# The last second product of the last MLP over 256, 128 and 128 tokens instead of 256 and 256

## The chip, the cores and the metric

The kernel runs on one core of a Trainium2 chip. The metric is the device time of one execution in microseconds (us), taken as the median of several runs. Before the change it is 2286.32 us (three runs, 2286.13 to 2287.78).

## The reference

Two layers over 1024 tokens of width 1024. The first mixes tokens by stick-breaking attention and a gated recurrence, the second by a convolution module; each is followed by an RMS-normed MLP with a squared ReLU, and a last RMS norm gives the output.

```python
def squared_relu_mlp(u, w1, w2):
    return jnp.square(jax.nn.relu(u @ w1)) @ w2
...
for layer in range(DEPTH):
    u = rmsnorm(h, norm_mix_g[layer])
    h = h + mixer(u)
    u = rmsnorm(h, norm_ffn_g[layer])
    h = h + squared_relu_mlp(u, w_ff1[layer], w_ff2[layer])
return rmsnorm(h, final_norm_g)
```

The MLP goes from 1024 to 4096 columns and back. The last norm needs, for each token, the sum of squares over all 1024 columns of the finished `h`.

## The kernel before

Activations lie transposed: 128 columns of the model on the partitions, tokens along the free dimension, so `h` is eight tiles `ht[hf][n]` (n = 0 to 7) of 128 x 512 for each half `hf` of the tokens. Every matrix is cut into panels of 128 output columns. `panel` (L100) loads one 512 KB panel into `wraw` (two buffers, queue of SyncE) and splits it into a rounded part and a remainder, `whl`: ScalarE writes the first (L110), VectorE the second (L111). `whl` has three buffers. Activations are split in the same way. `gemm` (L114) then makes three products for each of the 8 blocks of 128 rows of the contraction, L121 to L123, each of them a weight load of 128 x 128 and a matmul over the tokens; a whole panel is 24 matmuls. The same weights go in twice, at L121 and L122.

An MLP (`mlp`, L694) runs over its 32 hidden panels in four groups of eight: eight panels of the first product, then eight panels of the second product over the group's eight hidden tiles `hid`, each added into `ht` by VectorE. Only in the last MLP (layer 1, second half of the tokens), in its last group, the second product is different (L738 to L750): it goes over 256 tokens first and the other 256 after that. Panels 0 to 3 of its weights are split ahead of time into tiles of their own (`held`, tiles `w2`) and stay; panels 4 to 7 go through the three buffers of `whl`, and the second pass begins with 7, 6 and 5, which still lie there, and loads 4 a second time for its last place.

After each pass, `final` (L869) norms and writes these tokens. `colsum_sq` squares the tiles on ScalarE (`sq`, L193) and adds them on VectorE (`acc`, L195), all but the last square; `stats` (L125) sums over partitions by small matmuls against ones (L140, result `st`), makes 1/sqrt in a few small instructions on VectorE and GpSimd (L143 to L149) and spreads it over the partitions with matmuls against the identity (L153, result `stb`); a matmul of plain float32 operands is two records in the profile. Then VectorE scales each tile by norm and gain (L895) and ScalarE's queue issues its output DMA (L896). In the last pass GpSimd takes three of the eight tiles (L881, L892), with their DMAs on SyncE's queue, from a copy of `stb` (`rbc`, L885).

What stands in which order on an engine is decided by a scheduler when the program is built, with raised priority for splits, additions and the norm; each engine then runs its list strictly in order. DMA issues stand in the list of the engine that issues them.

Of the kernel before, what the change touches and what calls it, by code (L numbers as in the profile page):

```python
# [18 lines left out]
H = 512  # L19
KT = D // P  # L20
# [34 lines left out]
def kernel(  # L55
# [44 lines left out]
    def panel(src, n, hl=None):  # L100

        raw = wp.tile([P, KT * P], F32, tag="wraw", name="wraw", bufs=2)
        to = raw[:, :n]
        nc.sync.dma_start(to if len(src.shape) == 2 else to.rearrange("p (g c) -> p g c", g=src.shape[1]), src)
        if hl is None:
            t = wp.tile([P, 2, KT * P], F32R, tag="whl", name="whl")
            hl = t[:, 0], t[:, 1]
        hi, lo = hl
        with tc.high_priority(offset=PRIO):
            ACT.activation(hi[:, :n], raw[:, :n], AF.Copy)  # L110
            DVE.tensor_tensor(lo[:, :n], raw[:, :n], hi[:, :n].bitcast(F32), ALU.subtract)  # L111
        return hi, lo

    def gemm(ps, hl, mov, koff=0, start=True, stop=True):  # L114

        n = len(mov)
        whi, wlo = hl
        for k in range(n):
            c = slice((k + koff) * P, (k + koff + 1) * P)
            hi, lo = mov[k]  # L120
            PE.matmul(ps, whi[:, c], hi, start=start and k == 0, stop=False)  # L121
            PE.matmul(ps, whi[:, c], lo, start=False, stop=False)  # L122
            PE.matmul(ps, wlo[:, c], hi, start=False, stop=stop and k == n - 1)  # L123
# [79 lines left out]
    def utile(name):  # L203
        return up.tile([P, 2, H], F32R, tag="u", name=name)

    def parts(ts):
        return [(t[:, 0], t[:, 1]) for t in ts]
# [421 lines left out]
    def hs(hf):  # L629
        return lambda k: ht[hf][k]  # L630
# [42 lines left out]
    def mm():  # L673
        return late[3].tile([P, H], F32, tag="mm2", name="mm2", bufs=4) if late else \
            pm.tile([P, H], F32, tag="mm", name="mm")
# [18 lines left out]
    def mlp(layer, hf, u, last=None):  # L694

        held = {}
        w2 = lambda n, hl=None: panel(w_ff2[layer, n, :, f0 * P:(f0 + GF) * P], GF * P, hl)  # L700
        for f0 in range(0, FT, GF):
            hid = []
            for f in range(f0, f0 + GF):
                hl = panel(w_ff1[layer, f], D)
                ps = mm()
                gemm(ps, hl, u)
                with tc.high_priority(offset=PRIO):
                    if late:
                        t = late[0].tile([P, H], F32, tag="relu", name="relu")
                        hh = late[1].tile([P, 2, H], F32R, tag="hid", name="hid")  # L710
                        s = late[0].tile([P, H], F32, tag="sqr", name="sqr")
                    else:
                        t = wk.tile([P, H], F32, tag="raw", name="relu", bufs=2)
                        hh = utile("hid")
                        s = wk.tile([P, H], F32, tag="raw", name="sqr", bufs=2)
                    ACT.activation(t, ps, AF.Relu)  # L716
                    ACT.activation(hh[:, 0], t, AF.Square)  # L717
                    ACT.activation(s, t, AF.Square)  # L718
                    DVE.tensor_tensor(hh[:, 1], s, hh[:, 0].bitcast(F32), ALU.subtract)  # L719
                hid.append(hh)  # L720
                if last is not None and f >= FT - 4:
                    n = f - FT + 4
                    held[n] = [utile("w2").rearrange("p a b -> p (a b)") for _ in range(2)]
                    w2(n, held[n])
                yield
            if last is not None and f0 == FT - GF:
                break
            for n in range(KT):
                hl = w2(n)
                ps = mm()  # L730
                gemm(ps, hl, parts(hid))
                d = hs(hf)(n)
                with tc.high_priority(offset=PRIO):
                    DVE.tensor_tensor(d, d, ps, ALU.add)  # L734
                yield
        if last is None:
            return
        for q in range(2):  # L738
            tk = slice(q * H // 2, (q + 1) * H // 2)
            order = (7, 6, 5, 0, 1, 2, 3, 4) if q else range(KT)  # L740
            for n in order:
                if n > 3 and (q == 0 or n == 4):
                    held[n] = w2(n)
                ps = mm()[:, :H // 2]
                gemm(ps, held[n], [(hi[:, tk], lo[:, tk]) for hi, lo in parts(hid)])
                d = hs(hf)(n)[:, tk]
                with tc.high_priority(offset=PRIO):
                    DVE.tensor_tensor(d, d, ps, ALU.add)
                yield
            last(tk, order)  # L750
# [10 lines left out]
    def first_norm():  # L761
        assert all(("o", n) in done for n in range(KT))
        ms.append(mlp(0, 0, mlp_norm(0, 0)))
# [4 lines left out]
    for name in TOKENS.split():  # L768
        f, n = name[0], name[1:]
# [15 lines left out]
        else:  # L785
            f, n, hf = name[:-2], int(name[-2]), "ab".index(name[-1])
# [136 lines left out]
    steps(m)  # L923
    ug = norm(0, V_MIX + 8)
    m = mlp(0, 1, ub)
    steps(m, 8)
    ys = glu_conv(0, ug, m, 0)
# [3 lines left out]
    pw(cu, 0)  # L931
    ua = mlp_norm(1, 0)
    m = mlp(1, 0, ua)
    ys = glu_conv(1, ug, m, 3)
    cu = ln_silu(ys)
# [68 lines left out]
```

## Time and profile before

| what | value |
| --- | --- |
| median of three runs | 2286.32 us |
| the profiled execution, whole | 2286.64 us |
| its span, first to last instruction | 2284.9 us |
| TensorE matmul, busy | 2256.3 us, 99% |
| TensorE weight load, busy | 1893.1 us, 83% |
| VectorE, ScalarE, GpSimd, busy | 66%, 40%, 4% |
| mean granted TensorE clock | 0.997 |
| second product of the last group, 256 and 256 tokens | about 2227 to 2274.6 us of the span |

The profile names PE for TensorE's matmuls, PEld for its weight loads, DVE for VectorE, ACT for ScalarE, POOL for GpSimd; SPq and ACTq are DMA issues on the queues of SyncE and ScalarE. A row of the timeline gives the start in us, the length in us, the engine, the line, the operation, output<-input, sizes, and xN where N instructions that follow each other are merged; in brackets the idle time ahead of it and what ended it. A row of the groups gives busy time in us and mean ns of one instruction. A matmul's recorded length contains its way through the array, so matmuls overlap each other in the records; how fast they follow each other is read from their starts.

### The profile page before, as it was taken

How to read it: one execution, taken by the hardware profiler on the slowest of the kernel's cores; microseconds unless marked ns; L12 is line 12 of the kernel's file. 1: busy time of each engine (PE TensorE's matmuls, PEld its weight loads, DVE VectorE, ACT ScalarE, POOL GpSimd, SP SyncE). 2: the span in 40 equal slices, each digit the busy share in tenths (PEclk: the TensorE clock that was granted, in tenths of full speed). 3: DMA queues.
4: the chain of work that ended last, by engine and by line, in shares of the span. 5: the costliest groups of instructions: out<-in, count | busy, mean ns of one | idle time of the engine just before them, and what ended most of it. 6: DMA issues, size and time to landing. Idle time of an engine off the chain costs nothing.

```text
span 2284.9 us, 27492 instructions
## 1 busy us (share of the span) xinstructions
PE 2256.3 (99%) x10780; PEld 1893.1 (83%) x10780; DVE 1505.3 (66%) x2179; ACT 922.2 (40%) x1453; POOL 82.5 (4%) x167
## 2 busy tenths in 40 slices
PE   8999999998999999999999999999999999999998
PEld 7887888887888888888888888888888888888888
DVE  7776777777343453469999876899997646433343
ACT  6544444545442344342414353442324534342341
POOL 1100010100000000000000000000000000000000
PEclk9999999999999999999999999999999999999999
DMA  5221122422343333332333333232332332423241
GB/s 174 70 63 47 46 73 80 128 88 71 114 138 98 93 101 92 99 95 94 100 95 100 94 100 93 93 100 94 100 94 93 102 93 92 138 92 102 93 138 47
DMA packets 70832, 217.96 MB, mean 95 GB/s; under 512 B 7984, under 2 KB 14256, under 8 KB 70704
## 3 DMA queue, kind: packets, MB, share of 16 engines
q1 hardware_dynamic: 59216, 197.71, 27.7%
q10 hardware_dynamic: 10208, 16.41, 2.2%
q0 software_dynamic: 1280, 2.10, 0.4%
q8 instruction: 84, 1.38, 0.2%
q14 instruction: 44, 0.36, 0.0%
HBM read 205.70 MB, written 8.39 MB: 94 GB/s over the span
## 4 chain that ended last, share of the span: by engine, by line
PE 97%; DVE 2%; ACT 1%; issue 0%; DMA 0%; POOL 0%; SPq 0%; POOLq 0%; ACTq 0%
PE mm L121 27%; PE mm L122 27%; PE mm L123 27%; PE av L443 2%; PE wtr L434 1%; PE pa L121 1%; PE pa L123 1%; PE pa L122 1%; PE pg L122 1%; PE pg L123 1%; PE pg L121 1%; PE zs L540 1%; PE z L415 1%; PE z L414 1%; PE st L140 1%; DVE ke L421 0%
## 5 line engine op out<-in xcount | busy, mean ns | idle before, releaser
L111 DVE TENSOR_TENSOR whl<-wraw,whl 128x1024 fp32r<-128x1024 f32 (+2 forms) x371 | 445.7, 1201 | 322.9 <-ACT whl L110 319.1
L110 ACT ACTIVATE whl<-wraw 128x1024 fp32r<-128x1024 f32 (+2 forms) x371 | 385.2, 1039 | 645.2 <-PE mm L123 522.6
L121 PE MATMUL mm<-u,whl 128*128 128x512 f32 x1456 | 571.8, 394 | 8.9 <-ACT u L279 6.1
L122 PE MATMUL mm<-u,whl 128*128 128x512 f32 x1456 | 570.8, 392 | 0.0
L123 PE MATMUL mm<-u,whl 128*128 128x512 f32 x1456 | 569.8, 391 | 0.0
L121 PE MATMUL mm<-hid,whl 128*128 128x512 f32 (+1 forms) x1024 | 391.6, 383 | 0.0
L122 PE MATMUL mm<-hid,whl 128*128 128x512 f32 (+1 forms) x1024 | 391.3, 383 | 0.0
L123 PE MATMUL mm<-hid,whl 128*128 128x512 f32 (+1 forms) x1024 | 390.8, 383 | 0.0
L837 DVE SCALAR_TENSOR_TENSOR y<-a,vec,y 128x512 f32<-128x512 f32 x480 | 345.1, 750 | 4.2
L121 PEld LDWEIGHTS mm<-u,whl 128*128 128x128 f32 x1456 | 273.9, 188 | 65.5 <-ACT u L279 6.8
L122 PEld LDWEIGHTS mm<-u,whl 128*128 128x128 f32 x1456 | 274.0, 188 | 55.2 <-DVE u L280 1.2
L123 PEld LDWEIGHTS mm<-u,whl 128*128 128x128 f32 x1456 | 274.0, 188 | 54.9
L123 PEld LDWEIGHTS mm<-hid,whl 128*128 128x128 f32 x1024 | 192.5, 188 | 37.4
L121 PEld LDWEIGHTS mm<-hid,whl 128*128 128x128 f32 x1024 | 192.5, 188 | 37.3
L122 PEld LDWEIGHTS mm<-hid,whl 128*128 128x128 f32 x1024 | 192.5, 188 | 37.2
L734 DVE TENSOR_TENSOR ht<-ht,mm 128x512 f32<-128x512 f32 x120 | 82.3, 687 | 199.3 <-PE mm L123 199.1
L716 ACT ACTIVATE relu<-mm 128x512 f32<-128x512 f32 x128 | 76.5, 598 | 326.1 <-PE mm L123 325.8
L421 DVE TENSOR_TENSOR_SCAN ke<-ke 128x128 f32<-128x128 f32 (+5 forms) x64 | 86.4, 1353 | 24.9 <-POOL ke L418 24.7
L719 DVE TENSOR_TENSOR hid<-sqr,hid 128x512 fp32r<-128x512 f32 x128 | 87.7, 686 | 4.1 <-ACT sqr L718 4.1
L717 ACT ACTIVATE hid<-relu 128x512 fp32r<-128x512 f32 x128 | 79.6, 622 | 0.1
L718 ACT ACTIVATE sqr<-relu 128x512 f32<-128x512 f32 x128 | 79.6, 622 | 0.0
L145 POOL TENSOR_TENSOR st_r<-st_m,nhalf 128x4 f32<-128x4 f32 (+1 forms) x21 | 24.1, 1149 | 1229.2 <-DVE st_m L143 1229.2
(227 smaller groups left out, 2501.2 us busy)
## 6 DMA issues: line engine op xcount, KB each, us to landing
wraw<-w_ff SPq DMA_DIRECT2D x257, 512.0 KB, 3.5
wraw<-w_in SPq DMA_DIRECT2D x46, 512.0 KB, 3.5
wraw<-w_glu SPq DMA_DIRECT2D x32, 512.0 KB, 3.5
wraw<-w_pw SPq DMA_DIRECT2D x16, 512.0 KB, 3.5
xk<-xT SPq DMA_DIRECT2D x16, 256.0 KB, 5.1
oraw<-o_dram ACTq DMA_DIRECT2D x16, 256.0 KB, 3.3
ht<-xT ACTq DMA_DIRECT2D x16, 256.0 KB, 4.0
wraw<-w_out SPq DMA_DIRECT2D x8, 512.0 KB, 3.6
```

The source lines that it names most:

```text
L110: ACT.activation(hi[:, :n], raw[:, :n], AF.Copy)
L111: DVE.tensor_tensor(lo[:, :n], raw[:, :n], hi[:, :n].bitcast(F32), ALU.subtract)
L121: PE.matmul(ps, whi[:, c], hi, start=start and k == 0, stop=False)
L122: PE.matmul(ps, whi[:, c], lo, start=False, stop=False)
L123: PE.matmul(ps, wlo[:, c], hi, start=False, stop=stop and k == n - 1)
L421: DVE.tensor_tensor_scan(kr, kr, kr, 1.0, ALU.mult, ALU.min)
L716: ACT.activation(t, ps, AF.Relu)
L717: ACT.activation(hh[:, 0], t, AF.Square)
L718: ACT.activation(s, t, AF.Square)
L719: DVE.tensor_tensor(hh[:, 1], s, hh[:, 0].bitcast(F32), ALU.subtract)
L734: DVE.tensor_tensor(d, d, ps, ALU.add)
L837: DVE.scalar_tensor_tensor(y, a[:, j:j + H], w(j), y, ALU.mult, ALU.add)
```

## The change

The second pass over 256 tokens is cut in two passes over 128. Each has its own eight additions, norm and output DMAs. Panel 4 is loaded again for the end of the second pass, as before, and is then used first in the third; panel 5 is loaded again for the end of the third.

```diff
-        for q in range(2):
-            tk = slice(q * H // 2, (q + 1) * H // 2)
-            order = (7, 6, 5, 0, 1, 2, 3, 4) if q else range(KT)
+
+        for tk, order, loads in ((slice(0, H // 2), range(KT), (4, 5, 6, 7)),
+                                 (slice(H // 2, 3 * H // 4), (7, 6, 5, 0, 1, 2, 3, 4), (4,)),
+                                 (slice(3 * H // 4, H), (4, 7, 6, 0, 1, 2, 3, 5), (5,))):
             for n in order:
-                if n > 3 and (q == 0 or n == 4):
+                if n in loads:
                     held[n] = w2(n)
-                ps = mm()[:, :H // 2]
+                ps = mm()[:, :tk.stop - tk.start]
                 gemm(ps, held[n], [(hi[:, tk], lo[:, tk]) for hi, lo in parts(hid)])
                 d = hs(hf)(n)[:, tk]
```

The line numbers behind this place grow by one. The order of the instructions changes on three engines. On ScalarE, before, from the end of the first pass to the end of the program (`ht` 128x256 are this pass's and the last's tokens; DMAs are the outputs):

```order
L193 ACTIVATE sq<-ht 128x256 [waits DVE_49,Activation_49] x4
L110 ACTIVATE whl<-wraw 128x1024 [waits DMAHW2_49,PE_49]
L190 ACTIVATE acc<-ht 128x256 [waits DVE_49]
L193 ACTIVATE sq<-ht 128x256 [waits DVE_49,Activation_49]
L896 DMA outT<-ht 128x256 [waits DVE_49] x8
L193 ACTIVATE sq<-ht 128x256 [waits DVE_49,Activation_49] x6
L885 ACTIVATE rbc<-stb 128x256 [waits PE_49]
```

The same stretch of ScalarE's list after the change, from the first pass's last squares to the third pass's first squares:

```order
L193 ACTIVATE sq<-ht 128x256 [waits DVE_49,Activation_49] x4
L190 ACTIVATE acc<-ht 128x128 [waits DVE_49]
L193 ACTIVATE sq<-ht 128x128 [waits DVE_49,Activation_49]
L897 DMA outT<-ht 128x256 [waits DVE_49] x2
L110 ACTIVATE whl<-wraw 128x1024 [waits DMAHW2_49,PE_49]
L897 DMA outT<-ht 128x256 [waits DVE_49] x5
L897 DMA outT<-ht 128x256 [waits DMAHW3_49,DVE_49]
L193 ACTIVATE sq<-ht 128x128 [waits DVE_49,Activation_49] x6
L110 ACTIVATE whl<-wraw 128x1024 [waits PE_49]
L190 ACTIVATE acc<-ht 128x128 [waits DVE_49]
L193 ACTIVATE sq<-ht 128x128 [waits DVE_49,Activation_49]
```

The split of the reloaded panel 4 has moved from ahead of the second pass's squares to between the first pass's output DMAs, and a second such split, of panel 5, stands ahead of the third pass's squares; behind the last row shown follow eight output DMAs of 128 x 128, six squares, `rbc` and five output DMAs.

On VectorE, after the change, from the end of the second pass into the third (`mm_17681` is the second pass's last panel, 4; `mm_17758` and `mm_17784` are the third's first two, 4 and 7):

```order
L749 TENSOR_TENSOR ht<-ht,mm_17681 128x128 [waits PE_49]
L749 TENSOR_TENSOR ht<-ht,mm_17758 128x128 [waits PE_49]
L143 TENSOR_SCALAR st_m<-st 128x1 [waits PE_49]
L147 TENSOR_TENSOR st_t<-st_r 128x1 [waits Pool_49]
L111 TENSOR_TENSOR whl<-wraw,whl 128x1024 [waits DMAHW3_49,Activation_49]
L148 SCALAR_TENSOR_TENSOR st_t<-st_t,st_m 128x1 [waits DVE_49]
L149 SCALAR_TENSOR_TENSOR st_r<-st_t,st_r 128x1 [waits DVE_49]
L749 TENSOR_TENSOR ht<-ht,mm_17784 128x128 [waits PE_49]
L195 TENSOR_TENSOR acc<-acc,sq 128x128 [waits Activation_49]
L896 SCALAR_TENSOR_TENSOR ht<-ht,vec,stb 128x128 [waits PE_49]
```

The norm of the second pass is new here, inside the third pass, and the split of panel 5 stands in the middle of it. On TensorE the third pass takes its place between the second pass's last panel and the end of the program, with the second pass's `st` matmuls after 5 and after 24 of its 192 matmuls and the `stb` matmuls after 67 of them.

## The prediction

> **What bounds the kernel now.** I read the page first (busy shares, then the chain that ended last), then the busy time by stretches, then the timeline of the last 60 us, and last the groups by shape. The page's shares of busy time and its chain, by engine:
>
> ```profile
> PE 2256.3 (99%) x10780; PEld 1893.1 (83%) x10780; DVE 1505.3 (66%) x2179; ACT 922.2 (40%) x1453; POOL 82.5 (4%) x167
> ...
> PE 97%; DVE 2%; ACT 1%; issue 0%; DMA 0%; POOL 0%; SPq 0%; POOLq 0%; ACTq 0%
> ```
>
> TensorE is the bound. But "PE busy" cannot say what inside TensorE is the limit, matmul or weight load. So the next view is the busy time in three stretches: the first pass of the changed product, a stretch inside that pass, and one of ordinary 512-token products.
>
> ```profile
> core 0: us, PE busy (x) PEld busy (x) DVE busy (x) ACT busy (x) POOL busy (x), PEclk, DMA share, GB/s
> 2227.00:2250.20 23.20, 23.20 (x195) 23.17 (x194) 8.38 (x16) 6.37 (x12) 0.00 (x0) 1.00 0.10 30
> 2240.00:2248.00 8.00, 8.00 (x69) 8.00 (x68) 3.39 (x7) 1.89 (x4) 0.00 (x0) 1.00 0.01 2
> 2100.00:2110.00 10.00, 10.00 (x46) 8.29 (x45) 2.70 (x3) 5.04 (x8) 0.00 (x0) 1.00 0.36 104
> ```
>
> The pace with 512 tokens, from two rows of the timeline, eight matmuls apart:
>
> ```profile
> 2224.99 0.39 PE L121 MATMUL mm<-u,whl 128*128 128x512 f32 x1
> ...
> 2226.80 0.39 PE L123 MATMUL mm<-u,whl 128*128 128x512 f32 x1
> ```
>
> With 512 tokens a matmul comes every 1.81/8 = 0.226 us and the weight loader has pauses (8.29 of 10 us). With 256 tokens one comes every 23.2/194 = 0.120 us, half the work in a little over half the time, and the loader has no pause left: 8.00 of 8.00 us. So in the stage that the change touches, the loader is already as busy as the matmuls. The clock is fully granted (1.00).
>
> How fast do weight loads follow each other when the matmul is narrower still? The trace has matmuls over 128 columns and over 2, each with its own load of 128 x 128; first as the timeline has them, then the mean length of one from the groups by shape:
>
> ```profile
> 85.99 1.05 PE L582 MATMUL kv<-hi,kn 128*128 128x128 f32 x8
> 86.88 0.60 PE L434 MATMUL wtr<-identr,ke 128*128 128x128 f32 x4
> ...
> 106.79 0.61 PE L173 MATMUL stb<-identr,st_rr 128*128 128x128 f32 x4
> ...
> 626.74 0.72 PE L173 MATMUL stb<-identr,st_rr 128*128 128x128 f32 x5
> ...
> 2251.03 0.54 PEld L140 LDWEIGHTS st<-ones,acc 128*128 128x128 f32 x4
> ...
> 2251.48 0.19 PEld L121 LDWEIGHTS mm<-hid,whl 128*128 128x128 f32 x1
> ```
>
> ```profile
> L173 PE MATMUL stb<-identr,st_rr 128*128 128x128 f32 x88 | 12.0, 270 | 0.0
> ```
>
> Eight `kv` from 85.99 to the next group at 86.88 are 0.111 us each. The `stb` rows are rounded float32, as in the changed product: (0.72 - 0.27)/4 = 0.112, (0.61 - 0.27)/3 = 0.113. The four loads of `st` start within 2251.48 - 2251.03, 0.112 each, with a moving operand of only 2 columns. From 128 columns to 2 the pace doesn't move: 0.111 us is what a weight load costs when nothing else is the limit.
>
> **The change part by part.** *The matmuls.* The second pass was 8 panels x 24 = 192 matmuls over 256 tokens. Now it is 384 over 128: the same multiplications, but twice the weight loads. At 0.111 us they cost 42.6 us, where 192 x 0.120 = 23.0 us stood: **+19.6 us**, all on the path, since TensorE has no idle time there. Ends: a pace of 0.120, as now, would give 46.1 (+23.0); 0.067 gives 25.7 (+2.7), if only columns counted: 256 fewer took 0.226 to 0.120, and 128 fewer would take half of that difference again. I take 0.111, the pace that rows of this very width show.
>
> [...]
>
> *One more norm in the stream.* A norm over 128 tokens has half the `st` and `stb` records of one over 256 (6 instead of 12). The second pass's six now stand inside the stream: 6 x 0.111 = **+0.7 us**.
>
> *The tail.* After the last matmul the chain of waits runs through the last norm:
>
> ```profile
> 2274.62 0.42 DVE L748 TENSOR_TENSOR ht<-ht,mm 128x256 f32<-128x256 f32 x1 [1.49 <-PE mm L123]
> ...
> 2275.13 0.42 ACT L193 ACTIVATE sq<-ht 128x256 f32<-128x256 f32 x1 [2.46 <-DVE ht L748]
> ...
> 2275.60 0.61 PE L140 MATMUL st<-ones,sq 128*128 128x2 f32 x4 [0.68 <-ACT sq L193]
> ...
> 2276.49 0.71 POOL L145 TENSOR_TENSOR st_r<-st_m,nhalf 128x2 f32<-128x2 f32 x1 [5.89 <-DVE st_m L143]
> ...
> 2277.93 0.68 PE L153 MATMUL stb<-identr,st_r 128*128 128x128 f32 x4 [1.72 <-DVE st_r L149]
> 2278.65 0.38 ACT L885 ACTIVATE rbc<-stb 128x256 f32<-128x256 f32 x1 [3.10 <-PE stb L153]
> 2279.06 2.05 DVE L895 SCALAR_TENSOR_TENSOR ht<-ht,vec,stb 128x256 f32<-128x256 f32 x5 [1.28 <-ACT rbc L885]
> ...
> 2279.58 2.38 ACTq L896 DMA_DIRECT2D outT<-ht  x5
> ```
>
> The DMA engines in the last stretch, by the same columns as the stretches above:
>
> ```profile
> 2281.00:2282.00 1.00, 0.00 (x0) 0.00 (x0) 0.11 (x1) 0.00 (x0) 0.26 (x1) 0.50 1.09 380
> ```
>
> Ten microseconds lie between 2274.6 and the end at 2284.9. What half the width saves is read from groups of both widths:
>
> ```profile
> L416 ACT ACTIVATE ke<-z 128x256 f32<-128x256 f32 x16 | 6.1, 379 | 13.8 <-PE wtr L434 7.2 <-PE z L415 6.6
> ...
> L416 ACT ACTIVATE ke<-z 128x128 f32<-128x128 f32 x16 | 4.3, 270 | 2.3 <-PE z L415 2.0 <-PE mm L123 0.2
> ...
> L895 DVE SCALAR_TENSOR_TENSOR ht<-ht,vec,stb 128x256 f32<-128x256 f32 x13 | 5.3, 475 | 2.6 <-PE stb L153 1.3 <-ACT rbc L885 1.3
> ...
> L593 DVE SCALAR_TENSOR_TENSOR state<-state,tots,kv 128x128 f32<-128x128 f32 x16 | 5.5, 344 | 0.4
> ...
> L145 POOL TENSOR_TENSOR st_r<-st_m,nhalf 128x4 f32<-128x4 f32 x19 | 22.7, 1196 | 901.1 <-DVE st_m L143 901.1
> ...
> L145 POOL TENSOR_TENSOR st_r<-st_m,nhalf 128x2 f32<-128x2 f32 x2 | 1.4, 704 | 328.1 <-DVE st_m L143 328.1
> ```
>
> An ACT instruction saves 0.11 (two on the chain: square and `rbc`), a DVE one 0.13 (addition and the first scaling); the power on POOL loses (1.196 - 0.704)/2 = 0.25 per column; `st` and `stb` lose two records each, 0.44 together. That is 0.22 + 0.26 + 0.25 + 0.44 = 1.2. The outputs gain little more: five issues on ACT's queue take 2.38/5 = 0.48 each and not the 0.41 of the DVE, so the issues set the pace and their number is unchanged. The transfers, which fill the DMA engines in the stretch at 2281 (share 1.09), move half the bytes: 0 if each row of a partition costs the same as before, 0.7 if the last one no longer queues behind the others; I take 0.3. **Tail: -1.5 us**, between -0.8 and -2.2.
>
> *The second reload and its waits.* Panel 5 is loaded once more, 512 KB in 3.5 us by the row of DMA issues below, on a queue of SP with nothing behind it but the last outputs. The splits wait for a buffer, and both engines do them in order. Their lengths and the output phase of the first pass:
>
> ```profile
> 2253.58 1.06 ACT L110 ACTIVATE whl<-wraw 128x1024 fp32r<-128x1024 f32 x1 [2.39 <-PE mm L123]
> ...
> 2254.68 1.23 DVE L111 TENSOR_TENSOR whl<-wraw,whl 128x1024 fp32r<-128x1024 f32 x1 [0.47 <-ACT whl L110]
> ...
> 2259.63 3.22 DVE L895 SCALAR_TENSOR_TENSOR ht<-ht,vec,stb 128x256 f32<-128x256 f32 x8 [1.33 <-PE stb L153]
> ...
> 2260.14 4.47 ACTq L896 DMA_DIRECT2D outT<-ht  x8
> ```
>
> ```profile
> wraw<-w_ff SPq DMA_DIRECT2D x257, 512.0 KB, 3.5
> ```
>
> Panel 4's split stood ready after one panel; now panel 7 is needed again and the split waits for panel 5's buffer, three panels in, 9.3 us after the second pass begins (84 records x 0.111). The two output DMAs ahead of it on ACT end by 9.8; the split is done at about 13 (DVE scales the first pass's eight tiles first). It is wanted at 20: cover 7 us. Behind it on ACT wait six DMAs and the second pass's squares, until about 17, of a pass of 22.6 us.
>
> Panel 5's split waits for panel 4 in the third pass (3.1 us in); ACT until 4.2, and DVE, where it stands behind L147, from about 4.5 to 5.7. Only then follow L148 and L149, `st_r` at 6.1; TensorE wants it for `stb` after 67 matmuls and 4 small records, at 7.9. Cover 1.8 us; if it goes, TensorE stands still for the excess. Then eight DMAs hold ACT from 8.5 to 13.0 while three panels' squares collect, worked off by about 16, well ahead of the last panel's end at 22. **0 us.**
>
> *Sum*, against the profiled execution of 2286.6 us (span 2284.9 and 1.7 around it): +19.6 + 0.7 - 1.5 = +18.8, 2305.4. That execution lies 0.3 above the median, so **2305.1 us**, +0.82%.
>
> **The rivals.** (1) *Only the columns count*: the loads run fully ahead, 0.067 us per matmul. Then +2.7 + 0.7 - 1.5 = +1.9 us: 2288, not slower by what a measurement of this kernel can tell (0.2%, 4.6 us). It speaks for it that 512 to 256 tokens goes nearly in proportion (0.226 to 0.120); against it stand the rows at 0.111 with 128 and 2 columns and the loader without a pause. It decides from a pace below 0.074, where 384 of them plus 0.7 - 1.5 stay under 23.0 + 4.6. [...] (2) *Loads partly hidden*: L121 and L122 use the same weights, so if the second load were in part skipped or pulled ahead, the pace lies between, 0.089 in the middle: 34.2 us, +11.2 + 0.7 - 1.5 = +10.4, 2297. Against it: in the stretches above a load is recorded for each matmul (x194 beside x195), and the rows at 0.111 leave nothing hidden. [...] (3) *The third pass stalls*: the 1.8 us cover of `st_r` or the ACT queue's backlog is gone, and TensorE or the tail waits 2 to 6 us more: 2307 to 2311. For it: the whole norm and output of one pass now fall into a pass that has more queued work than before. Against: the third pass, bound by loads, is 22 us, hardly shorter than the second before (192 x 0.120 + 12 x 0.111 = 24.4).
>
> **How the numbers follow.** Forecast 0.80, (1) 0.04, (2) 0.07, (3) 0.09. The forecast's own range is 2303 to 2307: a pace of 0.108 to 0.115 is 1.3 either way, the tail 0.7. To hold 8 in 10 it reaches over most of case (3) and into nothing of (1): 2301 to 2309. Faster by over 0.2% 0.02, within 0.2% 0.03, both from (1); slower 0.95.
>
> **What would show it.** In the profile after: two groups of 192 records over 128x128 in `mm<-hid`, PE starts 0.11 us apart, about 43 us plus 2 us of small records from the second pass's start to the last matmul; no PE idle time at the `stb` matmul; DVE's L111 between L147 and L149; from the last matmul to the end about 8.8 instead of 10.3 us. It is wrong if those starts are 0.09 us apart or less, or if PE shows idle time in the third pass.

## The result, and the profile after

The changed kernel takes 2304.94 us (median of five runs, 2304.0 to 2307.23) against 2286.32 before (five runs, 2285.46 to 2287.78): a ratio of 1.0082, 95% interval 1.0072 to 1.0093, +18.6 us. The prediction was 2305.1.

The profiled execution after is the longest of the five (2307.23 us, span 2305.5): the second pass already starts 1.5 us later in it than in the profile before (first narrow matmul at 2251.57, against 2250.06 for the first of the second pass there), in work that the change doesn't touch. So the two profiles are compared from that start on: 2284.9 - 2250.1 = 34.8 us before, 2305.5 - 2251.6 = 53.9 after, +19.1.

Busy times of the whole span after, then by stretches: in the profile before the first and second pass, in the profile after the first, and the second and third together (columns as in the prediction's stretches).

```profile
PE 2280.1 (99%) x10972; PEld 1915.5 (83%) x10972; DVE 1509.8 (65%) x2206; ACT 925.2 (40%) x1462; POOL 82.1 (4%) x168
```

```profile
2226.80:2250.10 23.30, 23.30 (x195) 23.25 (x194) 8.38 (x16) 6.37 (x12) 0.00 (x0) 1.00 0.10 34
2250.10:2274.60 24.50, 24.50 (x209) 24.50 (x207) 10.82 (x27) 4.18 (x9) 2.59 (x4) 1.00 0.13 43
```

```profile
2228.20:2251.50 23.30, 23.30 (x195) 23.22 (x194) 8.37 (x16) 6.37 (x12) 0.00 (x0) 1.00 0.17 57
2251.50:2296.60 45.10, 45.10 (x406) 45.10 (x405) 16.71 (x54) 6.85 (x18) 2.55 (x5) 1.00 0.11 36
```

The first pass is unchanged. The second half of the tokens took 24.5 us and takes 45.1: +20.6 us, with TensorE busy and its loader busy all the time. The page's share of busy TensorE, 99% both times, shows nothing of this; its count of instructions does: 192 more. The pace, from two rows of the timeline eight matmuls apart, in panel 7, the first of the second pass:

```profile
2253.08 0.27 PE L122 MATMUL mm<-hid,whl 128*128 128x128 f32 x1
...
2253.97 0.28 PE L121 MATMUL mm<-hid,whl 128*128 128x128 f32 x1
```

That is 0.89/8 = 0.111 us for half the columns of a matmul that took 0.120.

The tail after the last matmul of the profile after, to be laid beside the tail in the prediction:

```profile
2296.61 0.29 DVE L749 TENSOR_TENSOR ht<-ht,mm 128x128 f32<-128x128 f32 x1 [1.67 <-PE mm L123]
...
2296.99 0.31 ACT L193 ACTIVATE sq<-ht 128x128 f32<-128x128 f32 x1 [2.37 <-DVE ht L749]
...
2297.36 0.38 PE L140 MATMUL st<-ones,sq 128*128 128x2 f32 x2 [0.61 <-ACT sq L193]
...
2298.02 0.56 POOL L145 TENSOR_TENSOR st_r<-st_m,nhalf 128x1 f32<-128x1 f32 x1 [5.52 <-DVE st_m L143]
...
2299.31 0.77 PE L153 MATMUL stb<-identr,st_r 128*128 128x128 f32 x2 [1.57 <-DVE st_r L149]
2300.11 0.28 ACT L886 ACTIVATE rbc<-stb 128x128 f32<-128x128 f32 x1 [2.81 <-PE stb L153]
...
2300.80 2.36 ACTq L897 DMA_DIRECT2D outT<-ht  x5
```

From the last addition's start to the end it is 8.9 us, before 10.3: -1.4 us. Every piece is shorter but one: two `stb` records take 0.77 us where four took 0.68. The granted clock (the column ahead of the last two) in half-microsecond stretches around that matmul, after and then before:

```profile
2297.50:2298.00 0.50, 0.24 (x2) 0.15 (x2) 0.16 (x1) 0.00 (x0) 0.00 (x0) 1.00 0.00 0
2298.00:2298.50 0.50, 0.00 (x0) 0.00 (x0) 0.00 (x0) 0.00 (x0) 0.48 (x1) 0.75 0.00 0
...
2299.50:2300.00 0.50, 0.50 (x2) 0.28 (x2) 0.00 (x0) 0.00 (x0) 0.00 (x0) 0.50 0.00 0
```

```profile
2278.00:2278.50 0.50, 0.50 (x4) 0.42 (x4) 0.00 (x0) 0.00 (x0) 0.00 (x0) 1.00 0.00 0
```

In the profile after, the clock has fallen to 0.50 by the time of `stb`; in the one before it is still 1.00 there.

### The profile page after: what moved, and what is told of

Same layout as the page of the kernel before. It is cut to its first block, busy times and chain, and to the rows that moved or that the text cites. A ratio compares the mean times of both kernels' runs of the same rounds, so it can differ in the third digit from the quotient of the medians.

```text
span 2305.5 us, 27943 instructions
## 1 busy us (share of the span) xinstructions
PE 2280.1 (99%) x10972; PEld 1915.5 (83%) x10972; DVE 1509.8 (65%) x2206; ACT 925.2 (40%) x1462; POOL 82.1 (4%) x168
## 4 chain that ended last, share of the span: by engine, by line
PE 97%; DVE 2%; ACT 1%; issue 0%; DMA 0%; POOL 0%; POOLq 0%; ACTq 0%
PE mm L121 27%; PE mm L122 27%; PE mm L123 27%; PE av L443 2%; PE wtr L434 1%; PE pa L121 1%; PE pa L123 1%; PE pa L122 1%; PE pg L122 1%; PE pg L123 1%; PE pg L121 1%; PE zs L540 1%; PE st L140 1%; PE z L415 1%; PE z L414 1%; PE stb L173 0%
## 5 line engine op out<-in xcount | busy, mean ns | idle before, releaser
L121 PE MATMUL mm<-hid,whl 128*128 128x512 f32 (+2 forms) x1056 | 400.1, 379 | 0.0
L122 PE MATMUL mm<-hid,whl 128*128 128x512 f32 (+2 forms) x1056 | 399.7, 379 | 0.0
L123 PE MATMUL mm<-hid,whl 128*128 128x512 f32 (+2 forms) x1056 | 399.4, 379 | 0.0
L123 PEld LDWEIGHTS mm<-hid,whl 128*128 128x128 f32 x1056 | 198.6, 188 | 37.5
L121 PEld LDWEIGHTS mm<-hid,whl 128*128 128x128 f32 x1056 | 198.6, 188 | 37.3
L122 PEld LDWEIGHTS mm<-hid,whl 128*128 128x128 f32 x1056 | 198.6, 188 | 37.3
L145 POOL TENSOR_TENSOR st_r<-st_m,nhalf 128x4 f32<-128x4 f32 (+2 forms) x22 | 24.5, 1116 | 1250.8 <-DVE st_m L143 1250.8
```

## The experiments

The theory, called L: in the narrow passes each matmul costs its weight load, 0.11 us, whatever it streams, so a pass cut in two pays 192 loads more. Its rivals: M, a fixed cost of any matmul; C, the columns still count; N, the added norm, reload and outputs, not the matmuls.

**e1: half of the tokens in the narrow passes.**

```diff
-                ps = mm()[:, :tk.stop - tk.start]
-                gemm(ps, held[n], [(hi[:, tk], lo[:, tk]) for hi, lo in parts(hid)])
-                d = hs(hf)(n)[:, tk]
+                tm = tk if tk.start == 0 else slice(tk.start, tk.start + 64)
+                ps = mm()[:, :tm.stop - tm.start]
+                gemm(ps, held[n], [(hi[:, tm], lo[:, tm]) for hi, lo in parts(hid)])
+                d = hs(hf)(n)[:, tm]
```

> The change, but in the two narrow passes the matmuls and the additions take only 64 of the 128 tokens; the rest of these tokens stays without the last second product. Loads are as many and as large as in the change. Theory L (each matmul costs its 128 x 128 weight load, 0.112 us, when it streams few columns): the time of the change, 2305 us, within 1 us. Theory M (each matmul costs a fixed 0.112 us of its own, whatever it loads): 2305 too. Theory C (the streamed columns still set the pace): 384 x 64 columns x 0.41 ns less, 10 us, so 2295 us.

Measured: 2342.29 us, ratio to the kernel before 1.0238 (1.0221 to 1.0255). All expectations missed: with half the streamed work the kernel is some 36 us slower than the change, each taken against the kernel before beside it. The timeline of e1 just after the narrow matmuls begin (at 2251.13), then its stretches:

```profile
2252.50 0.28 PE L121 MATMUL mm<-hid,whl 128*128 128x64 f32 x1
...
2254.18 0.28 PE L121 MATMUL mm<-hid,whl 128*128 128x64 f32 x1
...
2256.79 0.40 PE L122 MATMUL mm<-hid,whl 128*128 128x64 f32 x1
```

```profile
2235.00:2250.00 15.00, 15.00 (x127) 15.00 (x127) 6.32 (x14) 3.79 (x8) 0.00 (x0) 1.00 0.12 36
2250.00:2260.00 10.00, 10.00 (x78) 10.00 (x77) 1.79 (x8) 1.04 (x3) 0.70 (x1) 0.84 0.00 0
2270.00:2280.00 10.00, 10.00 (x48) 10.00 (x49) 0.86 (x4) 0.58 (x2) 0.00 (x0) 0.50 0.00 0
```

For the first 5.5 us the pace with 64 columns is 1.68/15 = 0.112 us (15 matmuls between the first two rows), the pace with 128: this much is as L and M said, and C falls. Then the granted clock goes from 1.00 to 0.50 and stays there, and each load takes 0.21 us (10/48), although TensorE works without a gap. That is another effect than the one under test; it is followed in e8 and e9.

**e2 and e3: half of the weight columns, with 128 and with 64 tokens.**

```diff
-            c = slice((k + koff) * P, (k + koff + 1) * P)
+            c = slice((k + koff) * P, (k + koff) * P + wc)
...
-                ps = mm()[:, :tk.stop - tk.start]
-                gemm(ps, held[n], [(hi[:, tk], lo[:, tk]) for hi, lo in parts(hid)])
-                d = hs(hf)(n)[:, tk]
+                wc = P if tk.start == 0 else 64
+                ps = mm()[:wc, :tk.stop - tk.start]
+                gemm(ps, held[n], [(hi[:, tk], lo[:, tk]) for hi, lo in parts(hid)], wc=wc)
+                d = hs(hf)(n)[:wc, tk]
```

e3 adds the cut of e1 to this.

> The change, but in the two narrow passes each matmul loads weights of 64 output columns instead of 128 and streams all 128 tokens; the upper half of each panel's output columns stays without the last second product. As many matmuls, loads half as large. Theory L: a load takes half, about 0.056 us, and the columns come to bound at about 0.067 us: 384 x (0.112 - 0.067) = 17 us less, 2288 us. Theory M: 2305 us. Theory N (the added norm, reload and output DMAs carry the loss, the matmuls don't): 2305 us, since they are all still there.

> Both cuts together: 64 weight columns and 64 tokens in the two narrow passes, the rest of these passes' sums left out. Theory L: a load of half the size at about 0.056 us bounds again (64 columns stream in about 0.041): 384 x 0.056 = 21.5 less, 2283 us. If a fixed cost of a matmul lies between (theory M in part), the pace stays at what e2 shows: 2288 us. Pure theory M: 2305 us.

Measured: e2 2287.78 us, ratio 1.0002 (0.9993 to 1.0011); e3 2287.54, 1.0003 (0.9993 to 1.0012). The same number of matmuls, norms, reloads and output DMAs as in the change costs next to nothing over the kernel before, once the loads are half as large. M and N fall with e2. The record of one load shortens too, from 192 ns in e4 (below; its loads are those of the change) to 135 in e2:

```profile
L122 PEld LDWEIGHTS mm<-hid,w 128*128 128x128 f32 x64 | 12.3, 192 | 0.0
```

```profile
L122 PEld LDWEIGHTS mm<-hid,w 128*64 128x64 f32 x64 | 8.7, 135 | 0.0
```

The edit halves the output rows of each matmul together with its load, so a cost that grows with the weight columns inside the matmul itself is not told apart from the load. The pace, 17 matmuls apart, first in e2 and then in e3:

```profile
2261.87 0.22 PE L122 MATMUL mm<-hid,whl 128*64 128x128 f32 x1
...
2262.89 0.22 PE L121 MATMUL mm<-hid,whl 128*64 128x128 f32 x1
```

```profile
2261.92 0.22 PE L121 MATMUL mm<-hid,w 128*64 128x64 f32 x1
...
2262.91 0.22 PE L123 MATMUL mm<-hid,whl 128*64 128x64 f32 x1
```

0.060 and 0.058 us: half of 0.112, and again nearly the same for 128 and 64 streamed columns, which L's bound of 0.067 by columns had not foreseen. e3's time was to fall to 2283 and didn't. Its loads did halve; most of what it misses lies behind them. From e2's chain of waits (start, length, what):

```profile
2272.98 1.47 DMA outT<-ht
2274.45 0.31 ACT sq L193
...
2275.92 0.30 DVE acc L195
2276.23 0.04 issue
2276.27 0.62 PE st L140 x4
```

ACT's queue is held by the second pass's output DMAs until 2274.4, the squares come late, and TensorE waits 2.25 us for the sum, in e3 2.4 us. This is the prediction's third rival, the stall: here, with half as long passes, it appears. That e2 hit its 2288 is therefore in part luck: 384 x (0.112 - 0.060) is 20.0 us where 17 was worked out, and the stall gives 2.25 back. Of the 4.5 us that e3 misses, 0.8 is the pace (0.058 for 0.056), 2.4 the stall, and 1.3 the kernel before, which took 2287.61 beside these runs and not 2286.32.

**e4: the matmuls of the change, but two norms.**

```diff
-            last(tk, order)
+            if tk.stop == H // 2:
+                last(tk, order)
+            elif tk.stop == H:
+                last(slice(H // 2, H), order)
```

> The second products over 256, 128 and 128 tokens as in the change, but only two norms and outputs of 256 tokens each, as before the change; both reloads stay. Theory L: the matmuls carry the loss; the tail is that of before again (+1.4) and six small records fewer stand in the stream (-0.7): 2305.6 us. Theory N: the third norm and its outputs were the loss: back to about 2286 us, plus what the reload costs.

Measured: 2307.27 us, ratio 1.0086 (1.0071 to 1.0101), +19.7 us over the runs of the kernel before beside it (2287.61). Without the third norm the loss is all there, so N falls a second time. The tail of e4 is 10.7 us in its profile where that of the change is 8.9, and it should be slower than the change by that much less six small records; the two intervals overlap, so the times alone don't show it.

**e5: 384 and 128 tokens.**

```diff
-        for tk, order, loads in ((slice(0, H // 2), range(KT), (4, 5, 6, 7)),
-                                 (slice(H // 2, 3 * H // 4), (7, 6, 5, 0, 1, 2, 3, 4), (4,)),
-                                 (slice(3 * H // 4, H), (4, 7, 6, 0, 1, 2, 3, 5), (5,))):
+        for tk, order, loads in ((slice(0, 3 * H // 4), range(KT), (4, 5, 6, 7)),
+                                 (slice(3 * H // 4, H), (7, 6, 5, 0, 1, 2, 3, 4), (4,))):
```

> Two passes as before the change, over 384 and 128 tokens. Theory L: a pass costs 192 times the larger of a load (0.112 us) and of the columns (0.226 us at 512 and 0.120 at 256 give 0.173 at 384): 33.2 + 21.4 = 54.6 us where 46.1 stood, +8.5; six more small records +0.7; the tail of 128 tokens -1.4: 7.8 us above the kernel before, 0.34%. If the loss of the change came from a third pass as such (its norm, its reload, its queue of outputs), two passes stay within 2 us of the kernel before.

Measured: 2294.78 us, ratio 1.0041 (1.0026 to 1.0056), +7.4 us. Two passes, no third norm, no further reload, and the loss is there in the size that the loads of one pass of 128 give. One of its nine executions took 2311.25 us (the others 2294.12 to 2295.53), and it is the one that the profile caught:

```profile
2240.00:2261.00 21.00, 21.00 (x128) 21.00 (x126) 6.69 (x11) 3.71 (x7) 0.00 (x0) 1.00 0.00 1
2261.00:2270.00 9.00, 9.00 (x59) 9.00 (x59) 2.65 (x8) 1.74 (x4) 1.32 (x2) 0.70 0.00 0
2270.00:2275.00 5.00, 5.00 (x26) 5.00 (x25) 1.58 (x4) 0.00 (x0) 0.00 (x0) 0.50 0.03 9
```

The clock halves as in e1, here with 128 columns, some 4.8 us into the narrow pass (2259.80 to about 2264.6), in which twelve small matmuls over 2 columns also stand.

**e6: one pass over 512 tokens**, with the norm of the narrow form.

```diff
-        for tk, order, loads in ((slice(0, H // 2), range(KT), (4, 5, 6, 7)),
-                                 (slice(H // 2, 3 * H // 4), (7, 6, 5, 0, 1, 2, 3, 4), (4,)),
-                                 (slice(3 * H // 4, H), (4, 7, 6, 0, 1, 2, 3, 5), (5,))):
+        for tk, order, loads in ((slice(0, H), range(KT), (4, 5, 6, 7)),):
...
-        if w < H:
+        if w < H or hf:
```

> One pass over all 512 tokens with the norm of the narrow form, then one tail. Theory L with the tail priced by width: matmuls 192 x 0.226 = 43.4 instead of 46.1 us (-2.7), no small records in the stream (-1.3), the tail longer by about 0.5 (addition and square), 0.9 (small matmuls), 0.5 (power), 0.5 (copy and first scaling) and 2.1 (GpSimd's three tiles) plus up to 2.7 for twice the output bytes: +4.5 to +7; together 0.5 to 3 us above the kernel before. If a narrow last pass were worth what its tail saves, without a price in matmuls, it would lose 4.5 to 7 us.

Measured: 2287.71 us, ratio 1.0002 (0.9993 to 1.0011). From its chain of waits, the first and the last pieces of the tail:

```profile
2269.94 0.70 DVE ht L747
...
2274.50 1.38 PE stb L153 x8
...
2279.14 1.22 POOL ht L891
```

Its tail is 2285.1 - 2269.9 = 15.2 us, 4.9 more than that of 256 tokens, and its matmuls and small records give 3.9 of that back: from the first matmul of the second product to the last addition it takes 2269.94 - 2226.22 = 43.7 us, where 2274.62 - 2227.03 = 47.6 stood. In the medians no loss is left that can be measured. The cut at 256 that the kernel already had gains nothing that can be measured over none.

**e7: a version meant to beat both.** Panels 0 to 3 over 512 tokens, 4 to 7 over 256 and 256.

```diff
+        halves = (slice(0, H // 2), slice(H // 2, H))
+        for tks, order in (((slice(0, H),), range(4)), (halves[:1], range(4, KT)), (halves[1:], (7, 6, 5, 4))):
+            for tk in tks:
+                for n in order:
+                    if n > 3 and tk.start == 0:
+                        held[n] = w2(n, held[0] if n == 7 else None)
...
+                if tk.stop - tk.start < H:
+                    last(tk, range(KT) if tk.start == 0 else (0, 1, 2, 3, 7, 6, 5, 4))
...
-            nc.scalar.dma_start(out[:, k, hf * H + tk.start:hf * H + tk.stop], o)
+            (nc.sync if w < H and tk.stop < H else nc.scalar).dma_start(
+                out[:, k, hf * H + tk.start:hf * H + tk.stop], o)
```

> A version meant to be faster than both: panels 0 to 3 over all 512 tokens at once, only panels 4 to 7 over 256 and 256; panel 7 is split into the tile of panel 0, so nothing is loaded twice; the outputs of the first 256 tokens go through SyncE's queue. Theory L: 96 x 0.226 + 192 x 0.120 = 44.7 us instead of 46.1, 1.4 us below the kernel before, if the first norm still hides, in the 11.5 us of the last four panels. If it doesn't hide (its scalings and squares queue ahead of the last additions), 2 to 5 us above the kernel before.

Measured: 2286.97 us, ratio 0.9999 (0.999 to 1.0008): no difference that can be measured. From its chain of waits:

```profile
2275.15 0.35 DVE acc L195
...
2275.63 1.04 PE st L140 x8
...
2278.38 1.20 PE stb L153 x4
```

The matmuls gain nearly what was expected, 1.3 us: the last matmul of the first product starts 1.4 us later than in the profile before (2228.20, there 2226.80), the last one of the second product 0.1 later (2274.42, there 2274.30). But a late sum now goes ahead of the last `st`, and `stb` takes 1.20 us instead of 0.68 (the granted clock averages 0.88 from 2270 to 2280); the tail is 11.2 us instead of 10.3, and most of the gain is given back.

**e8 and e9: 96 and 112 tokens in the narrow passes**, otherwise as e1.

> Like e1 with 96 of the 128 tokens in the two narrow passes (the other 32 stay without the last second product), to see at which width the granted clock falls as it did with 64. If the clock follows the share of time in which columns stream (48% with 128, 24% with 64, 36% here), either it stays at 1.00 and the time is that of the change, about 2306 us, or it falls to 0.50 and the time is that of e1, about 2342 us.

> Like e1 and e8 with 112 of the 128 tokens in the two narrow passes (the other 16 stay without the last second product): columns stream for 42% of a load's 0.112 us, between e8 (36%, the clock fell) and e3 (64 columns in 0.0593 us, 45%, it stayed). The clock stays at 1.00 and the time is that of the change, about 2306 us, or it falls to 0.50 and the time is about 2342 us; a mixture over several executions would put the point of change near here.

Measured: 2341.35 us (one execution) and 2340.89 (two, ratio 1.0239, 1.0209 to 1.0269). Stretches of e9 about the fall:

```profile
2250.00:2260.00 10.00, 10.00 (x70) 10.00 (x68) 1.84 (x8) 1.00 (x3) 0.70 (x1) 0.74 0.00 0
2260.00:2270.00 10.00, 10.00 (x49) 10.00 (x48) 5.04 (x13) 1.68 (x3) 0.00 (x0) 0.50 0.31 107
```

The clock falls with 112 columns as with 64, to the same 0.50 and nearly the same time (2340.89 us, in e1 2342.29).

## Why the prediction was right

- **The matmuls, +19.6 us.** Right. The pace is 0.111 as taken from `kv` and `stb`; over the whole stretch 45.1 us for 384 matmuls and 18 small records is 0.112 each. With the six small records the prediction had +20.3; the stretches give +20.6. e1's first 5.5 us show the pace without regard to the columns; e2 and e3 that it follows the size of the load, 0.112 to 0.060; e4 and e5 that the loss is in the number of narrow matmuls and not in the third norm or reload. That the number and size of the weight loads set the loss is thereby shown; the one thing left open is the split between the load and a cost of the matmul that grows with its weight columns (e2).
- **The tail, -1.5 us.** The sum is right (-1.4), some of its terms are not. Addition, square, `st` and the copy shrank as taken (by 0.13, 0.11, 0.23 and 0.10). The power on POOL lost 0.15, not 0.25 (0.71 to 0.56). `stb` was to lose 0.22 and gained 0.09, because the clock had fallen to 0.50. The outputs made up for it: from the copy's end to the end of the span 5.1 us after and 5.9 before, 0.8 less, where the first scaling and the transfers were taken at 0.4. That these misses, 0.4 one way and 0.3 the other, nearly cancel is luck.
- **The second reload and its waits, 0 us.** Right. The rows of the third pass in the profile after, VectorE first:

```profile
2278.42 0.16 DVE L147 TENSOR_TENSOR st_t<-st_r 128x1 f32<-128x1 f32 x1 [0.66 <-POOL st_r L145]
2278.50 1.22 DVE L111 TENSOR_TENSOR whl<-wraw,whl 128x1024 fp32r<-128x1024 f32 x1
2279.64 0.15 DVE L148 SCALAR_TENSOR_TENSOR st_t<-st_t,st_m 128x1 f32<-128x1 f32 x1
2279.83 0.16 DVE L149 SCALAR_TENSOR_TENSOR st_r<-st_t,st_r 128x1 f32<-128x1 f32 x1
...
2282.23 0.43 PE L153 MATMUL stb<-identr,st_r 128*128 128x128 f32 x2
...
2283.08 4.09 ACTq L897 DMA_DIRECT2D outT<-ht  x8
```

  The split stands in the middle of the norm and delays `st_r` to 2280.0; `stb` follows at 2282.2 with no wait in its row, a cover of 2.2 us where 1.8 was worked out. ACT is free of outputs at 2287.2, 9 us ahead of the last matmul.
- **The rivals.** Columns alone (0.067) and partly hidden loads (0.089) are refuted by the pace of 0.111. The stall of the third pass didn't come: with passes of some 22 us its work was done in time, and with half as long ones, in e2 and e3, it wasn't.

What the prediction had no word of is how near the change, with 128 columns, lies to the fall of the clock (to 0.50 with 112, e9), which cost some 36 us more in e1, e8 and e9. In the profile of the change the clock is 1.00 through all three passes, and the mean clocks of its other four executions (0.995 to 0.997, against 0.980 in e9) leave no room for it, so it didn't touch the forecast. That it would stay away was not foreseen but lucky: e5 has 128 columns too, and one of its nine executions fell.

## What to carry to other kernels

Price a cut along the streamed side by the number of weight loads, and take their pace from the narrowest matmuls that the trace has: here cutting from 256 columns to 128 halved the work of a matmul and took its time only from 0.120 to 0.111 us. A shorter tail is worth what the tail's own pieces lose, here 1.4 us of 10.3, since its chain of small instructions and DMA issues hardly shrank with the tile (five issues took 2.36 us for half the bytes, where 2.38 stood). And look at the granted clock of a narrow stage before trusting "busy": in e9 TensorE and its loader show no pause from 2260 to 2270 (10.00 of 10 us each) and run at a clock of 0.50.

## What the runs showed of the hardware that was not expected

With full loads of 128 columns and TensorE without a gap, the granted clock fell to 0.50 with 64, 96 and 112 streamed columns, and stayed at 1.00 with 128 in the profile of the change. It fell 5.6 us after the narrow matmuls began in e1 (2251.13 to about 2256.7, by the clock of 0.85 from 2256 to 2257) and 5.7 in e8 (2249.90 to about 2255.6, by 0.81 from 2255 to 2256); in e9 it is 0.74 in the mean of 2250 to 2260 and 0.50 after that. At 0.41 ns a column, an estimate (0.226 less 0.120 us over 256), columns stream for 24, 36 and 42% of a 0.112 us load in the cases that fell, for 47% with 128, and for 45% in e3 (64 columns in 0.058 us), which didn't fall. So in e1, e3, e8, e9 and the profile of the change the lower shares go with the fall; that the share decides was not shown, and a cause was not isolated.

A limit can't be read from these shares, because small matmuls over 2 columns stand among the narrow ones ahead of every fall. In e5 they are these:

```profile
2260.53 0.78 PE L140 MATMUL st<-ones,acc 128*128 128x2 f32 x6
...
2263.21 0.78 PE L140 MATMUL st<-ones,sq 128*128 128x2 f32 x6
```

The change and e1, e3, e8 and e9 have eight in the same places. With them, an estimate from the paces above gives 20, 30 and 35% from the first narrow matmul to the fall in e1, e8 and e9 (e9 taken with the delays of the other two), 34% in e5's one execution that fell, and 40 and 38% over the first 5.5 us in the change and in e3, which held. e5's one execution so fits that order, but eight of its nine have the same matmuls and didn't fall; what decides between them is not known.

A load of 64 columns paces at 0.058 us and one of 128 at 0.112: by these two points an estimate of 0.84 ns for each weight column and some 4 ns besides.
